# A decoder trunk on one core: two rows of a head's values moved behind the scores, and another order of the short and the long product in every wide block

## The chip, the cores and the metric

The kernel runs on one core of a Trainium2 chip. The metric is the device time of one execution in microseconds (us), as the median of several runs. Lower is better. The engines are named as the profile names them: PE is TensorE (its matmuls), PEld its weight loads, DVE is VectorE, ACT is ScalarE, POOL is GpSimd, SP is the engine whose queue issues most of the transfers.

## What is computed

A trunk of two layers over 256 tokens of width 1024, all in float32. Layer 0 mixes the tokens with a gated short convolution, layer 1 with dilated window attention (three groups of eight heads of 128, with partial rotary embedding). Each layer then has a squared-ReLU MLP (1024 to 4096 and back) and a gated per-layer input. Cut to what matters:

```python
for i in range(DEPTH):                                   # DEPTH = 2
    hn = rmsnorm(h, norm_mix[i])
    mixed = short_conv_mixer(...) if i == 0 else dilated_attention_mixer(hn, positions, w_qkv, w_o)
    h = h + mixed
    h = h + squared_relu_mlp(rmsnorm(h, norm_mlp[i]), mlp_w_up[i], mlp_w_down[i])
    h = h + sigmoid(rmsnorm(h, norm_ple[i]) @ ple_w_gate[i]) * (p[i] @ ple_w_proj[i])
return rmsnorm(h, norm_final)

def dilated_attention_mixer(h, positions, w_qkv, w_o):   # 3 groups g, 8 heads, 128 wide
    q, k, v = split(h @ w_qkv); q, k = partial_rotary(q), partial_rotary(k)
    for g: scores over a dilated window, softmax, times v, log of the sum
    return (softmax over the groups of those logs, times the outputs, summed) @ w_o
```

## The kernel before

Every float32 operand is split into a high and a low part of type fp32r, and a product of two such operands is made of three products: low weight by high activation, high weight by high activation, high weight by low activation. The weights stream from HBM in slabs (`raw`), ACT rounds a slab to its high part (`whi`, L368), DVE subtracts that to get the low part (`wlo`, L307), several slabs ahead of their use.

The work stands in a plan, a list that `make_plan` writes out by hand. An entry is a block of products of one 128x128 weight tile (or one slice of a row of them) or a step ("do") such as the rotary embedding or the softmax. `block` issues the matmuls of one entry (L404). There are three kinds:

- `"w"`, a *wide* block, is two matmuls. The weights are stationary. One streams the 256 columns of the activation's high part against `wlo` (below: the *short product*, S, a row with 128x256). The other streams 512 columns, high part and low part side by side, against `whi` (the *long product*, L, 128x512). The two halves of the bank are added up later by `add_up`, with one ACT and one DVE instruction for each half of a pair.
- `"n"` is three short products, all of 256 columns, for the few places that add up nothing later.
- `"t"` has the activations stationary and streams weight columns, 384 of them for a head's values (`acc_v`, a row with 128x384), 512 in the last stage.

Wide blocks come in twos, `half` 0 and 1 (the two column tiles of a pair of 128). Before the change the order of the two products follows `half`: S L for 0, L S for 1, so a stretch of wide blocks reads S L L S S L L S. Only the first group's queries and keys (g = 0) of heads 1 to 7 have S L in both halves:

```python
products = products[::-1] if half and (key != "qkv" or col[1] or not col[2]) else products
```

Head h of the attention is, in the plan: queries and keys of group 0 (`acc_qk`, 16 wide blocks); `scores` of head h-1, with the products of head h-2's values (`sc`, `o`, `tp` are the tiles of scores, of probabilities times values, and of the transposed probabilities); groups 1 and 2 of the queries and keys; `turn`, which transposes the probabilities of head h-1; eight rows of products for the values of head h (`v(h, ks)`, k from 0 to 7, six products of 384 columns each), with `qk_out` of group 2 and `qk_split` between them; `v_out`, which empties the two banks of the values. Head 1 differs: its `scores` come at group 2 and its `turn` behind the values ("late"). Head 7's scores come between blocks of the output projection (`w_o`).

PSUM has eight banks in one pool; a wide block's pair takes two, a head's values two, the scores two. Instructions run on each engine in the order that a scheduler gives them, which follows the plan, with a priority for some steps.

Of the kernel before, what the change touches and what calls it, by code (L numbers as in the profile page):

```python
# [18 lines left out]
NK = D // P  # L19
NP = NK // 2  # L20
FF = 4 * D
# [120 lines left out]
def make_plan():  # L142
    plan = [("do", "begin")]
    plan += proj_plan()

    def conv_in(what, c, ks):
        s = "BCX".index(what)
        return [
            ("w" if c and (what, c) != ("B", 3) or what == "X" else "n", "sc_in", k, s * NK + 2 * c + i, (what, c), i, "x0")
            for k in ks for i in (0, 1)  # L150
        ]


    for kp in range(NP):
        for what in "CBX":
            plan += conv_in(what, 0, (2 * kp, 2 * kp + 1))
            if what == "C" and kp + 1 < NP:
                plan.append(("do", "x_in", kp + 1))
            if what == "B":
                plan.append(("do", "squares", 0, kp))  # L160
    plan.append(("do", "add_up", ("X", 0)))
    for c in range(1, NP):
        plan += conv_in("C", c, range(2))
        plan += [("do", "stat", 0)] if c == 1 else []
        plan += conv_in("C", c, range(2, NK)) + ([("do", "add_up", ("C", c))]) + conv_in("X", c, range(3))
        plan += [("do", "spread", 0), ("do", "conv", 0)] if c == 1 else []
        plan += conv_in("X", c, range(3, NK)) + [("do", "add_up", ("X", c))] + conv_in("B", c, range(NK))
        plan.append(("do", "conv", c))

    def mix(key, j, ks):  # L170
        return [("w", key, k, 2 * j + i, ("o", j), i, "y") for k in ks for i in (0, 1)]

    for k in range(6):
        plan += mix("sc_out", 0, (k,)) + mix("sc_out", 1, (k,))

    plan += mix("sc_out", 2, range(3))
    for j in range(NP):
        plan += mix("sc_out", j, range((6, 6, 3, 0)[j], NK)) + [("do", "mix_out", 0, j)]
    plan += mlp_plan(0) + gate_plan()

    plan.append(("do", "masks"))

    def qk(h, g, ks):
        return [
            ("w", "qkv", k, (i, g, h), ("qk", h, g), i, "x3") for k in ks for i in (0, 1)
        ]

    def v(h, ks):
        return [("t", "v", k, h, ("v", b, h), b, "x3") for k in ks for b in (0, 1)]

    for kp in range(NP):
        for g in range(GROUPS):
            for k in (2 * kp, 2 * kp + 1):
                plan += qk(0, g, (k,))
                if (k, g) == (NK - 2, 0):
                    plan.append(("do", "stat", 3))
    plan += [("do", "add_up", ("qk", 0, g)) for g in (2, 0, 1)]
    plan += v(0, (0, 1)) + [("do", "spread", 3)]
    plan += [("do", "qk_out", 0, g) for g in (2, 0, 1)] + v(0, range(2, NK)) + [("do", "v_out", 0)]

    for h in range(1, HEADS):

        late, scores, turn = h == 1, [("do", "scores", h - 1)], [("do", "turn", h - 1)]
        for g in range(GROUPS):
            plan += qk(h, g, range(3)) + ([("do", "qk_out", h, g - 1)] if g else []) + qk(h, g, range(3, NK))
            if g == 0:
                plan += [("do", "qk_split", 0)] if late else scores
            elif g == 2:
                plan += scores if late else turn
            plan += [("do", "add_up", ("qk", h, g))]  # L210
        plan += v(h, range(2)) + [("do", "qk_out", h, 2)] + v(h, range(2, 4)) + [("do", "qk_split", h)]
        plan += v(h, range(4, NK)) + (turn if late else []) + [("do", "v_out", h)]

    last = HEADS - 1

    def w_o(kj):

        return [
            ("w" if j < 3 else "n", "w_o", k, 2 * j + i, ("o", j), i, "y") for k, j in kj for i in (0, 1)
        ]  # L220


    plan += w_o((k, j) for k in range(5) for j in (0, 1)) + [("do", "scores", last)]
    plan += w_o([(5, 0), (5, 1)] + [(k, 2) for k in range(6)] + [(0, 3), (1, 3)]) + [("do", "turn", last)]
    plan += w_o((k, 3) for k in range(2, 6)) + [("do", "last_values")]
    for j in range(NP):
        plan += w_o([(6, j), (7, j)]) + [("do", "mix_out", 1, j)]
    plan += mlp_plan(1) + [("do", "last_load")] + last_plan()
    return plan
# [36 lines left out]
def tile_trunk(ctx: ExitStack, tc: tile.TileContext, plan, slabs, ap, out):  # L266
# [51 lines left out]
    h = [held("h", f"h{j}", NP + 1) for j in range(NP)]  # L318
    state = {k: {} for k in ("u", "y", "p0", "p1", "qk", "pT", *(f"x{n}" for n in range(6)))}
    acc, left, opened = {}, {}, set()  # L320
    for op in plan:
        if op[0] != "do":
            key = ((*op[4], op[5]), 0) if op[0] == "w" else (op[4], op[5] if op[0] == "n" else 0)
            left[key] = left.get(key, 0) + 1
    rstd, rows, cur, mask, by_token = {}, {}, {}, {}, {}

    def gain(n, k):
        return gains[:, n * NK + k : n * NK + k + 1]
# [2 lines left out]
    offsets, n = [], 0  # L331
# [47 lines left out]
    def block(kind, key, k, col, name, half, operand, m=0, cuts=1):  # L379
        name = (*name, half) if kind == "w" else name  # L380
        if name not in opened:
            acc[name] = bank("acc_" + "_".join(map(str, name)))
        left[name, half if kind == "n" else 0] -= 1
        whi, wlo = weights((key, k, col))
        x = state[operand][k // 2]
        if kind == "n":
            dst = acc[name][:, half, :]
            products = ((dst, wlo, x[0][:, k % 2, :]), (dst, whi, x[1][:, k % 2, :]), (dst, whi, x[0][:, k % 2, :]))

            products = (products[2], products[0], products[1]) if key == "proj0" else products  # L390
        elif kind == "w":

            dst = acc[name]
            products = ((dst[:, 0, :], wlo, x[0][:, k % 2, :]), (flat(dst), whi, flat(x[2][:, k % 2, :, :])))

            products = products[::-1] if half and (key != "qkv" or col[1] or not col[2]) else products
        else:
            n = width(key) * P // cuts
            whi, wlo = (t[:, m * n : (m + 1) * n] for t in (whi, wlo))
            dst = flat(acc[name])[:, :n]  # L400
            xhi, xlo = (t[:, k % 2, half * P : (half + 1) * P] for t in x[:2])
            products = ((dst, xhi, whi), (dst, xhi, wlo), (dst, xlo, whi))
        for n, (to, a, b) in enumerate(products):
            nc.tensor.matmul(  # L404
                to,
                a,
                b,
                start=n == 0 and name not in opened,
                stop=n == len(products) - 1 and left[name, half if kind == "n" else 0] == 0,
                skip_group_check=True,  # L410
            )
            opened.add(name)
# [269 lines left out]

    def scores(head):

        weights = cur["pr", head] = pair(f"sm{head}", dtype=F32)[2]
        ps = [psum.tile([P, 512], F32, tag="ps", name=f"sc{head}_{b}") for b in (0, 1)]
        rest = values(head - 1) if head else None
# [265 lines left out]
```

## Time and profile before

| | |
|---|---|
| median of 3 runs | 771.32 us (771.22 to 771.48) |
| the profiled execution | 771.19 us |
| its span in the trace | 769.4 us |
| PE busy | 761.2 us (99%), 4716 matmuls |
| DVE busy | 598.6 us (78%) |
| ACT busy | 488.7 us (64%) |
| POOL busy | 8.9 us (1%) |
| moved from HBM | 138.97 MB read |

A matmul's row in the timeline has its start, its duration and its tiles. Matmuls are pipelined, so durations overlap: an S lasts 0.28 us and an L 0.40 us in the rows, but the next one starts earlier. What counts for the time is the distance from one start to the next start, called the *pitch* below. It is read from two rows of the timeline and the count of matmuls between them.

### The profile page before, as it was taken

To read this page: it belongs to the slowest core of one execution; us is meant where nothing else is said; L and a number is where in the kernel's file an instruction comes from. 1 tells how busy PE (TensorE), PEld (TensorE's weight loads), DVE (VectorE), ACT (ScalarE), POOL (GpSimd) and SP (SyncE) were. 2 spreads that over 40 slices of the span, in tenths; PEclk is the share of its full clock that TensorE was granted. 3 is DMA by queue.
4 is the path that set the end of the run, shared out by engine and by line. 5 is a ranking of instruction groups with operands and counts; after the bars stand their busy time and mean duration, and the time that the engine had idled before them with its cause. 6 is when DMAs were issued, how large, how long until landed. Compare 5 with 4: busy or idle time off the path is not lost.

```text
span 769.4 us, 12415 instructions
## 1 busy us (share of the span) xinstructions
PE 761.2 (99%) x4716; PEld 680.2 (88%) x4716; DVE 598.6 (78%) x967; ACT 488.7 (64%) x796; POOL 8.9 (1%) x22
## 2 busy tenths in 40 slices
PE   9999999999999999999999999999999999999996
PEld 9988888888888899989989989989988888888885
DVE  6898789898566668898988978977899887655564
ACT  7765566666444446688887778777666555444453
POOL 0000000000000000000000000000000000000002
PEclk9999999999999999999999999999999999999999
DMA  8855555556555554554555456456465555555521
GB/s 311 312 190 192 195 191 169 190 190 197 188 190 191 192 191 139 191 187 152 169 171 197 152 162 200 147 160 219 138 192 188 193 191 191 187 188 189 184 90 56
DMA packets 42539, 140.83 MB, mean 183 GB/s; under 512 B 4848, under 2 KB 6384, under 8 KB 42480
## 3 DMA queue, kind: packets, MB, share of 16 engines
q1 hardware_dynamic: 41904, 139.39, 54.3%
q8 instruction: 37, 0.61, 0.3%
q10 hardware_dynamic: 576, 0.66, 0.3%
q14 instruction: 22, 0.18, 0.1%
HBM read 138.97 MB, written 1.05 MB: 182 GB/s over the span
## 4 chain that ended last, share of the span: by engine, by line
PE 97%; issue 1%; DMA 1%; DVE 0%; POOL 0%; SPq 0%; POOLq 0%; ACT 0%; DVEq 0%
PE acc_u L404 23%; PE acc_d L404 23%; PE acc_qk L404 18%; PE acc_v L404 9%; PE acc_o L404 6%; PE acc_g L404 5%; PE acc_B L404 3%; PE acc_C L404 3%; PE acc_X L404 3%; PE acc_p L404 1%; PE o L736 1%; PE sc L692 1%; PE o L746 1%; DMA raw<-in_w 1%; PE sc L700 1%
## 5 line engine op out<-in xcount | busy, mean ns | idle before, releaser
L307 DVE TENSOR_TENSOR wlo<-raw,whi 128x1024 fp32r<-128x1024 f32 (+2 forms) x277 | 319.2, 1155 | 126.4 <-ACT whi L368 123.9
L368 ACT ACTIVATE whi<-raw 128x1024 fp32r<-128x1024 f32 (+2 forms) x277 | 277.9, 1007 | 166.2 <-PE acc_d L404 77.1
L404 PE MATMUL acc_u<-x,whi 128*128 128x512 f32 x512 | 160.8, 396 | 0.0
L404 PE MATMUL acc_d<-u,whi 128*128 128x512 f32 x512 | 160.8, 395 | 0.0
L404 PE MATMUL acc_qk<-x,whi 128*128 128x512 f32 x384 | 124.6, 395 | 0.0
L404 PEld LDWEIGHTS acc_d<-u,wlo 128*128 128x128 f32 x512 | 96.2, 188 | 22.7
L404 PEld LDWEIGHTS acc_u<-x,wlo 128*128 128x128 f32 x512 | 96.0, 188 | 22.5
L404 PE MATMUL acc_u<-x,wlo 128*128 128x256 f32 x512 | 101.3, 278 | 0.0
L404 PE MATMUL acc_d<-u,wlo 128*128 128x256 f32 x512 | 100.9, 278 | 0.0
L404 PE MATMUL acc_qk<-x,wlo 128*128 128x256 f32 x384 | 86.9, 280 | 0.0
L404 PEld LDWEIGHTS acc_qk<-x,wlo 128*128 128x128 f32 x384 | 72.1, 188 | 12.1
L404 PEld LDWEIGHTS acc_u<-x,whi 128*128 128x128 f32 x512 | 78.0, 189 | 0.2
L404 PEld LDWEIGHTS acc_d<-u,whi 128*128 128x128 f32 x512 | 77.9, 189 | 0.0
L404 PE MATMUL acc_v<-whi,x 128*128 128x384 f32 x256 | 67.2, 337 | 0.0
L404 PEld LDWEIGHTS acc_qk<-x,whi 128*128 128x128 f32 x384 | 62.5, 188 | 4.6
L404 PEld LDWEIGHTS acc_v<-whi,x 128*128 128x128 f32 x256 | 46.5, 188 | 0.1
L404 PE MATMUL acc_v<-wlo,x 128*128 128x384 f32 x128 | 42.9, 335 | 0.0
L423 ACT ACTIVATE r<-acc_u 128x256 f32<-128x256 f32 x64 | 24.1, 378 | 27.8 <-PE acc_u L404 27.5
L404 PE MATMUL acc_o<-y,whi 128*128 128x512 f32 (+1 forms) x144 | 41.0, 370 | 0.0
L655 ACT ACTIVATE rot<-qk 16x512 f32<-16x512 f32 x48 | 30.3, 632 | 9.9 <-DVE qk L424 9.2
L424 DVE TENSOR_TENSOR r<-acc_u,r 128x256 f32<-128x256 f32 x64 | 26.5, 419 | 3.5 <-ACT r L423 3.0
L404 PEld LDWEIGHTS acc_o<-y,wlo 128*128 128x128 f32 x128 | 24.0, 188 | 5.0
(175 smaller groups left out, 976.4 us busy)
## 6 DMA issues: line engine op xcount, KB each, us to landing
raw<-in_w SPq DMA_DIRECT2D x230, 512.0 KB, 3.6
raw<-in_w SPq DMA_DIRECT2D x32, 384.0 KB, 3.4
raw<-in_w SPq DMA_DIRECT2D x10, 256.0 KB, 4.9
h<-in_xT SPq DMA_DIRECT2D x4, 256.0 KB, 5.0
gain<-in_gain SPq DMA_DIRECT2D x2, 256.0 KB, 4.6
out<-htg SPq DMA_DIRECT2D x2, 256.0 KB, 2.1
mask<-in_mask SPq DMA_DIRECT2D x2, 192.0 KB, 3.4
raw<-in_w ACTq DMA_DIRECT2D x2, 128.0 KB, 3.7
```

Of the source, the lines that this page charges most:

```text
L307: nc.vector.tensor_tensor(out, a, f32(b), ALU.subtract)
L368: nc.scalar.activation(hi[:, :width], t[:, :width], AF.Copy)
L404: nc.tensor.matmul(to, a, b, start=n == 0 and name not in opened, stop=n == len(products) - 1 and left[name, half if kind == "n" else 0] == 0,
L423: nc.scalar.activation(t[:, i, :], p[:, 1, :], AF.Copy)
L424: nc.vector.tensor_tensor(t[:, i, :], p[:, 0, :], t[:, i, :], ALU.add)
L655: nc.scalar.activation(r[dst : dst + 16], p[src : src + 16], AF.Copy)
L692: nc.tensor.matmul(ps[b][:, :S], q[:, 0, own], k[:, 1, :], start=n == 0, stop=n == 2)
L700: nc.tensor.matmul(ps[b][r * 64 : (r + 1) * 64, at : at + 64], t[:, 0, of], t[:, 1, of], start=True, stop=True)
L736: nc.tensor.matmul(ps[:, 0, :], a, b[:, kb, :], start=kb == 0 and n == 0, stop=False, skip_group_check=True)
L746: nc.tensor.matmul(ps[to, 0, q], v12[:, b, r * P + m * 64 : r * P + (m + 1) * 64], t[:, b, r * 64 : (r + 1) * 64], start=False, stop=n == ...
```

## The change

It does four things.

1. `block` keeps a counter `wide_run`. A wide block with counter 0 issues S L; every later one issues L S. A block of kind `"n"` and the step `scores` set the counter to 0, a block of kind `"t"` sets it to a large number. So behind short products a stretch reads S L, L S, L S, L S: one pair of neighbours in opposite orders, and then alternation. Behind a head's values it reads L S, L S from the start.
2. From head 2 on, the rows k = 0 and 1 of a head's values move from behind group 2 to directly behind `scores`, ahead of group 1. Head 1 keeps them where they were.
3. `qk_out` of group 2 now stands behind row 2 and `qk_split` behind row 4 of the values (before: behind rows 1 and 3).
4. `add_up` of a group of queries and keys is asked for ahead of `scores` or `turn`, not behind.

```diff
         for g in range(GROUPS):
             plan += qk(h, g, range(3)) + ([("do", "qk_out", h, g - 1)] if g else []) + qk(h, g, range(3, NK))
+            plan += [("do", "add_up", ("qk", h, g))]
             if g == 0:
-                plan += [("do", "qk_split", 0)] if late else scores
+
+                plan += [("do", "qk_split", 0)] if late else scores + v(h, range(2))
             elif g == 2:
                 plan += scores if late else turn
-            plan += [("do", "add_up", ("qk", h, g))]
-        plan += v(h, range(2)) + [("do", "qk_out", h, 2)] + v(h, range(2, 4)) + [("do", "qk_split", h)]
-        plan += v(h, range(4, NK)) + (turn if late else []) + [("do", "v_out", h)]
+        plan += (v(h, range(2)) if late else []) + v(h, (2,)) + [("do", "qk_out", h, 2)] + v(h, (3, 4)) + [("do", "qk_split", h)]
+        plan += v(h, range(5, NK)) + (turn if late else []) + [("do", "v_out", h)]
...
         x = state[operand][k // 2]
+        if kind != "w":
+
+            wide_run["n"] = 0 if kind == "n" else NK * FF
...
-            products = products[::-1] if half and (key != "qkv" or col[1] or not col[2]) else products
+
+            done = wide_run.get("n", 0)
+            wide_run["n"] = done + 1
+            products = products[::-1] if done % 2 or done > 1 else products
...
     def scores(head):
 
+        wide_run["n"] = 0
```

How it moves the rows of PE, at three places. First, inside the down projection of the MLP (`acc_d_1_0` and `acc_d_1_1` are the banks of the two halves, `u5` the activations, `whi85` and `wlo85` a slab's parts). Before:

```order
L404 MATMUL acc_d_1_0_2374<-u5_1592,wlo85_2295 128x256
L404 MATMUL acc_d_1_0_2374<-u5_1592,whi85_2294 128x512
L404 MATMUL acc_d_1_1_2383<-u5_1592,whi85_2294 128x512
L404 MATMUL acc_d_1_1_2383<-u5_1592,wlo85_2295 128x256
L404 MATMUL acc_d_1_0_2374<-u5_1592,wlo85_2295 128x256
L404 MATMUL acc_d_1_0_2374<-u5_1592,whi85_2294 128x512
L404 MATMUL acc_d_1_1_2383<-u5_1592,whi85_2294 128x512
L404 MATMUL acc_d_1_1_2383<-u5_1592,wlo85_2295 128x256
```

The same eight places after:

```order
L411 MATMUL acc_d_1_0_2374<-u5_1592,whi85_2294 128x512
L411 MATMUL acc_d_1_0_2374<-u5_1592,wlo85_2295 128x256
L411 MATMUL acc_d_1_1_2383<-u5_1592,whi85_2294 128x512
L411 MATMUL acc_d_1_1_2383<-u5_1592,wlo85_2295 128x256
L411 MATMUL acc_d_1_0_2374<-u5_1592,whi85_2294 128x512
L411 MATMUL acc_d_1_0_2374<-u5_1592,wlo85_2295 128x256
L411 MATMUL acc_d_1_1_2383<-u5_1592,whi85_2294 128x512
L411 MATMUL acc_d_1_1_2383<-u5_1592,wlo85_2295 128x256
```

No matmul is added or removed; two long products never stand next to each other now, nor two short ones. Second, PE where the convolution's output projection (`acc_o`) begins behind three-product blocks (`acc_B_3`), after the change:

```order
L411 MATMUL acc_B_3_945<-x0_3_376,whi34_846 128x256 x2
L411 MATMUL acc_o_0_0_1024<-y0_571,wlo35_870 128x256
L411 MATMUL acc_o_0_0_1024<-y0_571,whi35_869 128x512
L411 MATMUL acc_o_0_1_1033<-y0_571,whi35_869 128x512
L411 MATMUL acc_o_0_1_1033<-y0_571,wlo35_870 128x256
L411 MATMUL acc_o_1_0_1036<-y0_571,whi35_869 128x512
L411 MATMUL acc_o_1_0_1036<-y0_571,wlo35_870 128x256
L411 MATMUL acc_o_1_1_1039<-y0_571,whi35_869 128x512
L411 MATMUL acc_o_1_1_1039<-y0_571,wlo35_870 128x256
```

The first two blocks stand as before the change (S L L S), and from the third on every block reads L S. Third, PE behind the scores of head 2 (`sc2`), where head 3 goes on. Before:

```order
L700 MATMUL sc2_1_4247<-qk_2_2_4098 64x64 x2
L404 MATMUL acc_qk_3_1_0_4296<-x3_0_3093,wlo147_4131 128x256
L404 MATMUL acc_qk_3_1_0_4296<-x3_0_3093,whi147_4130 128x512
L404 MATMUL acc_qk_3_1_1_4305<-x3_0_3093,whi147_4130 128x512
L404 MATMUL acc_qk_3_1_1_4305<-x3_0_3093,wlo147_4131 128x256
```

After:

```order
L708 MATMUL sc2_1_4252<-qk_2_2_4100 64x64 x2
L411 MATMUL acc_v_0_3_4296<-whi147_4125,x3_0_3093 128x384
L411 MATMUL acc_v_0_3_4296<-wlo147_4126,x3_0_3093 128x384
...
L411 MATMUL acc_v_1_3_4306<-wlo147_4126,x3_0_3093 128x384
L411 MATMUL acc_v_1_3_4306<-whi147_4125,x3_0_3093 128x384
L411 MATMUL acc_qk_3_1_0_4316<-x3_0_3093,whi148_4148 128x512
L411 MATMUL acc_qk_3_1_0_4316<-x3_0_3093,wlo148_4149 128x256
```

Twelve products of the values (two rows) now stand between the 64-column matmuls of the scores and group 1, which begins with a long product.

More of the change, by code (lines that the diff above doesn't have):

```diff
@@ L324, in tile_trunk @@
             left[key] = left.get(key, 0) + 1
-    rstd, rows, cur, mask, by_token = {}, {}, {}, {}, {}
+    rstd, rows, cur, mask, by_token, wide_run = {}, {}, {}, {}, {}, {}
     def gain(n, k):
```

## The prediction

> **What bounds the kernel now.** I read the page first, for the engine that bounds, then the waits, then the timeline of PE for pitches. Lines of the page (busy time, granted clock, the chain that ended last):
>
> ```profile
> span 769.4 us, 12415 instructions
> PE 761.2 (99%) x4716; PEld 680.2 (88%) x4716; DVE 598.6 (78%) x967; ACT 488.7 (64%) x796; POOL 8.9 (1%) x22
> PEclk9999999999999999999999999999999999999999
> PE 97%; issue 1%; DMA 1%; DVE 0%; POOL 0%; SPq 0%; POOLq 0%; ACT 0%; DVEq 0%
> ```
>
> PE is the path from end to end, at full clock. Next, the waits: of PE alone (the first line is the whole answer), and two lines of the list for all engines (us in total, times, longest):
>
> ```profile
> PE warm L531 <- DVE power L527: 1.0, 1, 1.0
> ...
> DVE wlo L307 <- ACT whi L368: 123.9, 122, 2.7
> ACT whi L368 <- PE acc_d L404: 77.1, 46, 2.0
> ```
>
> PE waited visibly for another engine only before its first matmul. The weight splitters wait the other way round: DVE for ACT (123.9 us), ACT for PE to free a slab (77.1 us). So the time is the number of matmuls times their pitch, and a change of order is worth what it does to the pitch. How many blocks there are, from the groups by shape (count behind the x, then busy us and mean ns):
>
> ```profile
> L404 PE MATMUL acc_u<-x,whi 128*128 128x512 f32 x512 | 160.8, 396 | 0.0
> L404 PE MATMUL acc_d<-u,whi 128*128 128x512 f32 x512 | 160.8, 395 | 0.0
> L404 PE MATMUL acc_qk<-x,whi 128*128 128x512 f32 x384 | 124.6, 395 | 0.0
> ...
> L404 PE MATMUL acc_o<-y,whi 128*128 128x512 f32 x112 | 35.1, 395 | 0.0
> ...
> L404 PE MATMUL acc_X<-x,whi 128*128 128x512 f32 x64 | 20.1, 395 | 0.0
> ...
> L404 PE MATMUL acc_C<-x,whi 128*128 128x512 f32 x48 | 15.1, 395 | 0.0
> ...
> L404 PE MATMUL acc_B<-x,whi 128*128 128x512 f32 x32 | 10.1, 395 | 0.0
> ```
>
> Each wide block has one long product: 512 + 512 + 384 + 112 + 64 + 48 + 32 = 1664 blocks. Group 0 of heads 1 to 7 (7 x 16 = 112) alternates already; 1552 blocks get a new order.
>
> Now the pitches. The timeline's rows begin with start and duration in us. First the down projection of layer 0 (first row of it, first row behind it), then group 0 of heads 3 and 4, likewise, which are the stretches that alternate before the change:
>
> ```profile
> 191.34 0.28 PE L404 MATMUL acc_d<-u,wlo 128*128 128x256 f32 x1
> ...
> 280.51 0.28 PE L404 MATMUL acc_g<-x,wlo 128*128 128x256 f32 x1
> ...
> 385.47 0.33 PE L404 MATMUL acc_v<-whi,x 128*128 128x384 f32 x1
> 385.65 0.28 PE L404 MATMUL acc_qk<-x,wlo 128*128 128x256 f32 x1
> 385.76 0.40 PE L404 MATMUL acc_qk<-x,whi 128*128 128x512 f32 x1
> ...
> 391.20 0.51 PE L736 MATMUL o<-pT,v 128*128 128x256 f32 x3
> ...
> 413.84 0.28 PE L404 MATMUL acc_qk<-x,wlo 128*128 128x256 f32 x1
> ...
> 419.39 0.63 PE L736 MATMUL o<-pT,v 128*128 128x256 f32 x4
> ```
>
> S L L S: 256 blocks in 280.51 - 191.34 = 89.17 us, 348.3 ns a block. Alternation: 16 blocks in 5.55 us, both times, 346.9 ns a block (the rows' last digit leaves +-0.6). To sharpen that, the pitches of unmixed streams: short products alone (the gate of layer 0, 102 of them up to `acc_qk`) and long ones alone (45 in the last stage):
>
> ```profile
> 292.19 0.28 PE L404 MATMUL acc_g<-x,wlo 128*128 128x256 f32 x1
> ...
> 304.43 0.28 PE L404 MATMUL acc_qk<-x,wlo 128*128 128x256 f32 x1
> 304.55 0.63 PE L404 MATMUL acc_qk<-x,whi 128*128 128x512 f32 x2
> 305.02 0.39 PE L404 MATMUL acc_qk<-x,wlo 128*128 128x256 f32 x2
> ...
> 750.50 0.39 PE L404 MATMUL acc_p<-whi,p 128*128 128x512 f32 x1
> ...
> 760.70 0.28 PE L404 MATMUL acc_p<-whi,p 128*128 128x256 f32 x1
> ```
>
> S alone: 12.24 us / 102 = 120.0 ns. L alone: 10.20 us / 45 = 226.7 ns. Their sum is 346.7 ns, just what alternation shows: alternating costs nothing over the two streams by themselves, and S L L S costs 1.6 ns more, some bubble at its doubled neighbours.
>
> **The change, part by part.**
>
> *The order.* 1552 blocks x (348.3 - 346.7) = 2.5 us gained. By 346.9 it is 2.2 us, which is the low end of a full gain; I take 346.7, since the sum of two long stretches is measured more finely than 16 blocks. The counter starts again at nine places (four times in the first convolution blocks, at the convolution's output projection, the first queries, twice in the attention's output projection, at the MLP of layer 1), and each keeps one doubled pair, half of what a period S L L S has: 9 x 1.6 ns = 0.01 us.
>
> Here a page speaks against the change. The Trainium skill, "TensorE: Matmul & The Clock Gate", section "Back-to-back issue gap", gives the isolated gap of a warm matmul as N/2.4 + 2.5 ns, a function of the columns alone. By it an S and an L take 109 and 216 ns (an estimate from that page) in any order, the order is free, and this term would be 0 in place of -2.5 us. The rows disagree in size (120.0 and 226.7) and show two prices for two orders.
>
> *New borders in the heads.* From head 2 on (six heads) the 64-column matmuls of the scores are followed by a value product and not by an S. Both borders stand in the trace, the first in head 1, the second in head 3:
>
> ```profile
> 348.54 0.45 PE L404 MATMUL acc_v<-whi,x 128*128 128x384 f32 x1
> 348.82 0.34 PE L404 MATMUL acc_v<-wlo,x 128*128 128x384 f32 x1
> ...
> 393.79 0.39 PE L404 MATMUL acc_qk<-x,wlo 128*128 128x256 f32 x1
> 394.01 0.63 PE L404 MATMUL acc_qk<-x,whi 128*128 128x512 f32 x2
> ```
>
> The first value product takes 0.28 us to the next start, 0.10 over the 0.18 of 385.47 to 385.65; the first S takes 0.22, 0.10 over its 0.12. So the exchange costs 0, with 0.02 for the rounding. The border from values to a *long* product is new: 13 times (group 1 of heads 2 to 7, group 0 of heads 1 and 3 to 7, the output projection behind head 7). No row shows it. Above, it is bounded by the 0.10 us of the border from 64 columns (1.3 us in all); below by the border from values to S, which costs 0 (385.47, 385.65, 385.76: pitches 0.18 and 0.11). It is nearest to the latter, as the products ahead are the same: I take 0.01 each, 0.13 us.
>
> *Less time for the chains on DVE and ACT.* Only two rows less of values (12 x 0.175 = 2.1 us) stand between `turn` and the use of the transposed probabilities; between `qk_split` and the scores it is one row (1.05 us). How much room there is, from the list by tile (duration min/median/max, first and last start; head 3's stretch):
>
> ```profile
> L736 PE MATMUL o<-pT,v x6: 274/281/282, 419.4 to 420.0; 128*128 128x256 f32 x6
> ...
> L307 DVE TENSOR_TENSOR pT<-tp,pT x1: 684/684/684, 407.4 to 407.4; 128x512 fp32r<-128x512 f32 x1
> ...
> L307 DVE TENSOR_TENSOR qk<-qk,qk x1: 684/684/684, 408.7 to 408.7; 128x512 fp32r<-128x512 f32 x1
> ```
>
> The probabilities are ready at 408.1 and used at 419.4: 11.3 us, of which 9.2 stay. The split queries and keys are ready at 409.4 for scores near 420: 10.6, of which 9.5 stay. The softmax gets 2.1 us more before `turn`. Cost 0. The two banks of the values are held over groups 1 and 2 too: a head then opens 12 banks of 8 as before, in another order. `add_up` earlier in DVE's and ACT's order frees its banks earlier; behind it stand the softmax and the copy of the output, which have those 9 us and more. The slab with value rows 0 and 1 is loaded and split four slabs earlier and queries' slabs one later: same count, same bytes, the SP queue in the new order of use. Cost 0; if the cover of 9 us were gone, the scores' consumers on PE would wait.
>
> *One place where PE does wait.* At the MLP of layer 1, the pair of long products behind 553.94 takes 0.57 us to the next start, against 0.47 at 304.55:
>
> ```profile
> 553.78 0.28 PE L404 MATMUL acc_u<-x,wlo 128*128 128x256 f32 x1
> 553.94 0.73 PE L404 MATMUL acc_u<-x,whi 128*128 128x512 f32 x2
> 554.51 0.40 PE L404 MATMUL acc_u<-x,wlo 128*128 128x256 f32 x2
> ```
>
> It waits for the activations, which DVE makes from the last output projection. What PE gains between the two is waited for again: at most some 32 blocks (8 of `acc_o`, 24 of `acc_u`) x 1.6 ns = 0.05 us.
>
> **Sum.** -2.5 + 0.01 + 0.12 (six exchanges at 0.02) + 0.13 + 0.05 = -2.2 us. The profiled execution took 771.19 us (span 769.4 and 1.8 around it): 769.0. The median of the runs is 0.13 higher; I say 769.1.
>
> **The rivals.**
>
> 1. *The order is free, or the bubble comes back with the other order.* An S and an L have their pitch, the 1.6 ns belong to the stage and not to the order, and the alternating stretches are cheap because values stand ahead of them. Against it: in the same heads, groups 1 and 2 are S L L S, on the same operands. Result 0 plus borders: 771.3 to 771.6. Chance 0.07. (This is what the rule of the Trainium skill's TensorE page, above, would make of the change.)
> 2. *Only a part settles.* The statistics' matmuls inside the MLPs (two short ones between `acc_u` blocks) are followed by alternation without a doubled pair; if the stream stays disturbed there, the second half of the up projections and all of the down projections (768 blocks) gain nothing. 768 x 1.6 ns = 1.2 us are missing then: 770.3. Head 2's group 0 speaks against it, which alternates behind four transposes. Chance 0.07.
> 3. *Slower: alternation locks in behind short products.* Behind S alone (304.43 to 305.02) the S takes 120 ns and each L 235: 355 a block. In S L L S this is made good, since the second S of a pair is cheaper. If S 120 with L 235 repeats without end, 1328 blocks (all but groups 1 and 2 of heads 1 to 7, which follow values) cost 6.7 ns more: 8.9 us, less 0.4 for the others, 0.3 for the borders: 780.1. It turns into a loss at a mean block above 348.3 ns. For it: alternation is seen only behind values and transposes, never behind S. Against it: the one doubled pair comes first, and both entries that are seen fall to 346.9 within a head. Chance 0.06.
> 4. *A wait in the heads.* The 9 us of room would have to go, in six heads; it begins to cost when DVE falls that far behind. Each us over is 6 us in all. Chance 0.02, price 772 to 776.
>
> **How the numbers follow.** The forecast has 0.78. Its own range: from -2.5 with free borders (768.8) to -2.2 by the 16-block reading, with all borders at their upper bound (0.05 + 0.12 + 1.3: 770.6, which I think unlikely). With 0.3 for the runs' own spread, the range that is to hold 8 in 10 takes in rival 2 and the borders' bound, 768.4 to 770.9; rivals 1, 3 and 4 (0.15) stay out. A difference under 0.2% (1.5 us) can't be told from none: faster means below 769.8. Faster 0.76 (the forecast, less 0.02 for its upper end), same 0.16 (rivals 1 and 2 and those 0.02), slower 0.08 (rivals 3 and 4).
>
> **What the profile after would show.** The down projection's 256 blocks in 88.75 us (346.7 each) and not 89.17, in both layers: this decides between forecast and rivals 1 to 3, and 90.9 would be rival 3. The up projection's halves before and behind the statistics' matmuls apart: rival 2. From values to a long product: a pitch of the last value product near 0.17 and of the first L near 0.23, with 0.33 for the upper bound. PE still with one wait, before its first matmul; any other is rival 4. I am wrong if the state of the stream behind short products outlives one pair, or if the bubble belongs to something other than doubled neighbours.

## The result

The changed kernel took 777.19 us (median; 774.99 to 777.42) against 771.40 us for the kernel before on the same chip: 1.0070 times as long, 95% interval 1.0056 to 1.0084. Slower by 0.7%, where 769.1 us and a gain of 0.3% were forecast. Three of the four executions took 777.2 to 777.4 us and one 774.99. The profiled one, on which all stage times below rest, took 777.18 us.

From the page of the changed kernel, span, busy time, granted clock and the chain's shares:

```profile
span 775.4 us, 12420 instructions
PE 766.5 (99%) x4716; PEld 682.9 (88%) x4716; DVE 598.8 (77%) x967; ACT 484.0 (62%) x796; POOL 8.9 (1%) x22
PEclk9999999999999999999999999999999999999999
PE 93%; DVE 3%; issue 2%; ACT 1%; DMA 1%; POOL 0%; SPq 0%; POOLq 0%; DVEq 0%; ACTq 0%
```

PE has the same 4716 matmuls at the same clock, is as busy as before (99%), and the span is 6.0 us longer: mostly, the pitch grew. The down projections, first row of each and first row behind it, in layer 0 and in layer 1:

```profile
192.64 0.40 PE L411 MATMUL acc_d<-u,whi 128*128 128x512 f32 x1
...
283.09 0.28 PE L411 MATMUL acc_g<-x,wlo 128*128 128x256 f32 x1
...
648.09 0.40 PE L411 MATMUL acc_d<-u,whi 128*128 128x512 f32 x1
...
738.54 0.40 PE L411 MATMUL acc_g<-whi,x 128*128 128x512 f32 x1
```

256 blocks in 90.45 us, twice: 353.3 ns a block, where S L L S had 348.3 and the forecast had 346.7. Inside one of them, and then in group 1 of head 3, which follows values:

```profile
193.34 0.40 PE L411 MATMUL acc_d<-u,whi 128*128 128x512 f32 x1
193.58 0.28 PE L411 MATMUL acc_d<-u,wlo 128*128 128x256 f32 x1
193.70 0.40 PE L411 MATMUL acc_d<-u,whi 128*128 128x512 f32 x1
193.94 0.28 PE L411 MATMUL acc_d<-u,wlo 128*128 128x256 f32 x1
194.05 0.40 PE L411 MATMUL acc_d<-u,whi 128*128 128x512 f32 x1
194.28 0.28 PE L411 MATMUL acc_d<-u,wlo 128*128 128x256 f32 x1
194.40 0.40 PE L411 MATMUL acc_d<-u,whi 128*128 128x512 f32 x1
...
398.54 0.33 PE L411 MATMUL acc_v<-whi,x 128*128 128x384 f32 x1
398.71 0.39 PE L411 MATMUL acc_qk<-x,whi 128*128 128x512 f32 x1
398.94 0.28 PE L411 MATMUL acc_qk<-x,wlo 128*128 128x256 f32 x1
399.06 0.39 PE L411 MATMUL acc_qk<-x,whi 128*128 128x512 f32 x1
```

In the down projection the L takes 0.24, 0.24, 0.23 us and the S 0.12, 0.11, 0.12, and this cycle of three blocks (1.06 us) repeats to the end. Behind values an L takes 0.23 and an S 0.12 at once, and stays there: 31 blocks at 346.7 ns. So alternation has two cycles, a *fast* one (346.7) and a *slow* one (353.3), and a stretch keeps the one it falls into until something interrupts it. S L L S lies between them, at 348.3. The kind of products ahead doesn't settle which: the 106 blocks of the first convolution behind `spread` (36.77 us) are fast too, and group 0 of head 2, behind four transposes, was fast before the change (346.7 ns from its third block) and is slow after it. In the changed kernel's trace the long stretches in the slow cycle hold 1153 blocks (17 of the first convolution columns, 190 from the convolution's output projection to the MLP's statistics, 384 from there to the end of the down projection, 36 of the first queries, 15 in head 2, 126 and 385 in layer 1). 1153 x 5.0 ns (353.3 - 348.3) = 5.8 us. By the stages below, those that are slow throughout lost 5.7 us together and the attention's output projection 1.0, while the heads gained 0.4 and what stands ahead of the convolution's output projection 0.3; this makes the 6.0.

By stage, worked out from the starts of matmuls (us from a stage's first matmul to the next stage's; profiled executions; s and f are the cycle, - is S L L S):

| stage | before | after |
|---|---|---|
| convolution's output projection | 22.29 - | 22.60 s |
| up projection 0, ahead of / behind the statistics | 44.59 - / 44.83 - | 45.23 s / 45.46 s |
| down projection 0 | 89.17 - | 90.45 s |
| first queries and keys | 17.19 - | 17.39 s |
| heads 1 to 7 | 196.19 | 195.75 f (group 0 of head 2: s) |
| attention's output projection | 27.17 | 28.17 |
| up projection 1, ahead / behind | 44.76 - / 44.83 - | 45.52 s / 45.46 s |
| down projection 1 | 89.17 - | 90.45 s |

The attention's output projection is a second loss, 1.0 us. The list of PE's waits has a new line there, for half of it:

```profile
PE o L744 <- DVE pT L308: 0.5, 1, 0.5
```

### The profile page after: what moved, and what is told of

It reads as the page before. It is cut to its first block, busy times and chain, and to the rows that moved or that the text cites. A ratio compares the mean times of both kernels' runs of the same rounds, so it can differ in the third digit from the quotient of the medians.

```text
span 775.4 us, 12420 instructions
## 1 busy us (share of the span) xinstructions
PE 766.5 (99%) x4716; PEld 682.9 (88%) x4716; DVE 598.8 (77%) x967; ACT 484.0 (62%) x796; POOL 8.9 (1%) x22
## 4 chain that ended last, share of the span: by engine, by line
PE 93%; DVE 3%; issue 2%; ACT 1%; DMA 1%; POOL 0%; SPq 0%; POOLq 0%; DVEq 0%; ACTq 0%
PE acc_u L411 23%; PE acc_d L411 23%; PE acc_qk L411 17%; PE acc_v L411 8%; PE acc_g L411 5%; PE acc_o L411 4%; PE acc_B L411 3%; PE acc_C L411 3%; PE acc_X L411 3%; DVE wlo L308 1%; PE acc_p L411 1%; PE o L744 1%; PE sc L700 1%; PE o L754 1%; DMA raw<-in_w 1%
## 5 line engine op out<-in xcount | busy, mean ns | idle before, releaser
L411 PE MATMUL acc_u<-x,whi 128*128 128x512 f32 x512 | 181.1, 399 | 0.0
L411 PE MATMUL acc_d<-u,whi 128*128 128x512 f32 x512 | 181.0, 399 | 0.0
L411 PE MATMUL acc_u<-x,wlo 128*128 128x256 f32 x512 | 143.8, 281 | 0.0
L411 PE MATMUL acc_d<-u,wlo 128*128 128x256 f32 x512 | 143.8, 281 | 0.0
L411 PE MATMUL acc_qk<-x,whi 128*128 128x512 f32 x384 | 134.2, 393 | 0.0
L411 PEld LDWEIGHTS acc_d<-u,whi 128*128 128x128 f32 x512 | 96.2, 188 | 24.0
L411 PEld LDWEIGHTS acc_u<-x,whi 128*128 128x128 f32 x512 | 96.1, 188 | 24.1 <-DVE x L455 0.2
L411 PE MATMUL acc_qk<-x,wlo 128*128 128x256 f32 x384 | 107.6, 280 | 0.0
L411 PE MATMUL acc_o<-y,wlo 128*128 128x256 f32 x128 | 35.7, 283 | 0.0
L683 ACT ACTIVATE v<-acc_v,n 64x128 f32<-64x128 f32 x64 | 23.2, 362 | 12.4 <-DVE v L679 11.7
```

The lines of the kernel that those rows point to most:

```text
L411: nc.tensor.matmul(to, a, b, start=n == 0 and name not in opened, stop=n == len(products) - 1 and left[name, half if kind == "n" else 0] == 0,
L683: nc.scalar.activation(v12[to, b, r * P : (r + 1) * P], p[own, g * P : (g + 1) * P], AF.Copy, scale=scale[own])
```

## The experiments

All ratios are to the kernel before on the same chip, with 95% intervals. The theories are first those that the result suggested, then the one that remained. In the expectations o0 and o1 are the output projections of the convolution and of the attention, and pT7 is the tile of head 7's transposed probabilities.

**The moved rows without the order.** After's plan, before's rule of order:

```diff
-            products = products[::-1] if done % 2 or done > 1 else products
+            products = products[::-1] if half and (key != "qkv" or col[1] or not col[2]) else products
```

> The change of the plan alone (value rows behind the scores, add_up and qk_split moved), with the order of products of before: S L L S everywhere, S L in group 0. Theory A (alternation of short and long products has two states, 346.7 and 353.3 ns a block; the changed kernel is in the slow one in the output projections, the MLPs and the first queries; the move costs nothing): 771.0 to 771.7 us, ratio 0.999 to 1.001, down projections at 89.17 us. Theory B (the moved rows or the waits behind them make the loss): 774 us or more.

Measured: 771.29 us, 1.0001 (0.9992 to 1.0010); behind the first matmuls of the convolution no stage of its trace differs from before by more than 0.02 us. The move alone costs nothing, in the heads and in the output projection.

**The doubled pair.** Three rules in place of after's: S L everywhere but behind values (no pair), L S everywhere, and two pairs ahead of the alternation.

```diff
-            products = products[::-1] if done % 2 or done > 1 else products
+            products = products[::-1] if done >= NK * FF else products      # e2
+            products = products[::-1] if True else products                 # e3
+            products = products[::-1] if done % 2 or done > 3 else products # e4
```

> As the changed kernel, but behind short products (and behind head 7's scores) every block is S L from the first on: no doubled pair. Theory A with the state set by the stream of short products ahead, whatever follows: 353.3 ns a block again, 90.45 us a down projection, 776.5 to 777.5 us. Theory A with the state set by the doubled pair L L: 346.7 ns, 88.75 us a down projection, 768.5 to 770 us. Rival (S L and L S differ as such, whatever stands ahead): the fast state wherever S L stands, the slow one nowhere, 768.5 to 770 us, and group 0 behind values no different from before.

> As the changed kernel, but every wide block is L S, with no doubled pair behind short products. Theory A, state set by the short products ahead: 353.3 ns a block, 776.5 to 777.5 us. Theory A, state set by the doubled pair: 346.7 ns, 768.5 to 770 us. Either way the heads behind values stay at 346.7.

> As the changed kernel, but with two doubled pairs (S L L S S L L S) behind short products before L S goes on. If the number of matmuls between the last short product and the alternation decides the state (a phase that each doubled pair shifts): the fast state, 346.7 ns, 88.75 us a down projection, 768.5 to 770 us. If the doubled pair has no part in it: 353.3 ns, 776.5 to 777.5 us as the changed kernel.

Measured: 774.16 us, 1.0050 (1.0031 to 1.0068); 777.25, 1.0074 (1.0059 to 1.0089); 775.33, 1.0055 (1.0040 to 1.0070). The whole MLP of layer 0 is in the slow cycle in all three: no pair, one or two at its start, S or L first, makes no difference there. But layer 1 differs, so that the totals of e2 and e4 lie in neither of the ranges expected. Its down projection is fast in e2 and e4, slow in e3. The two down projections of e2:

```profile
192.98 0.28 PE L411 MATMUL acc_d<-u,wlo 128*128 128x256 f32 x1
...
283.43 0.28 PE L411 MATMUL acc_g<-x,wlo 128*128 128x256 f32 x1
...
646.75 0.28 PE L411 MATMUL acc_d<-u,wlo 128*128 128x256 f32 x1
...
735.49 0.40 PE L411 MATMUL acc_g<-whi,x 128*128 128x512 f32 x1
```

The same instructions on the same shapes, 90.45 us and 88.74 us. So the cycle isn't fixed by the order, the shapes or the kind of stream ahead alone. In layer 1 the up projection can begin behind a wait of PE for the activations (0.2 us in e3); no trace has such a wait in layer 0. The executions of one kernel differ as well: 774.02 to 777.62 us in e2, 775.53 to 777.75 in e3, 774.99 to 777.42 after the change, where those of the kernel before lie within 1.1 us in each comparison. From the statistics of layer 1 to the end of its down projection the slow cycle costs 2.5 us over the fast one (45.46 + 90.45 against 44.61 + 88.75, in e3 and e2), so layer 1 falling now into one, now into the other would fit; each kernel has one profile, so this is not shown. What remained was a theory: the cycle depends on *when*, within the cycle, a stretch is entered, and an interruption can shift it.

**Added products of other widths.** `kick` issues a few matmuls whose output is not used; the stretch behind it begins with L.

```diff
+    def kick():
+        wide_run["n"] = NK * FF
+        ps = flat(bank("kick"))
+        for _ in range(N):
+            nc.tensor.matmul(ps[:, :W], ones_r, cur["slab"][:, :W], start=True, stop=True)
```

It stands ahead of the convolution's output projection, behind `spread` of that mixer (e5 to e8), ahead of the first queries (e9 to e12), behind the statistics of both MLPs, and ahead of the MLP of layer 1. Each run has its kick at all of its five places.

> The changed kernel with one extra product of 384 columns (its result is not used) at five places: ahead of the convolution's output projection, behind the spread of the first statistics, behind the statistics inside each MLP, ahead of layer 1's MLP; L S from there. Theory A1 (the state is set by the kind of stream ahead, and a product longer than its weight load puts it in the fast state): up projections behind the statistics 44.6 us and down projections 88.75 us in both layers, -7.2 us and +0.9 for the extra products, 770.5 to 771.5 us. Theory A2 (the state hangs on the exact distance in time, whatever the kind): some stretches fast, some slow, 771 to 777 us.

> As the kernel with one extra product of 384 columns, but three in a row at each of the five places (+2.6 us). A1: all five stretches fast, 772 to 773 us, the down projections 88.75 us. A2: mixed again, and not the same stretches as with one.

> Three extra products of 512 columns at each of the five places (+3.4 us). A1: all fast as behind 384 columns, 773 to 774 us. If the head's values do it by 384 columns alone and not by length: slow or mixed, 775 to 780.5 us.

> Three extra short products (256 columns) at each of the five places (+1.8 us), the control. A1: slow, as behind other short products: the down projections 90.45 us, 778 to 779.5 us. A2 or any disturbance will do: some or all fast, 771.5 to 777 us.

> The changed kernel with one extra product of 128 columns (result not used) at five places: ahead of the convolution's output projection, of the first queries, of layer 1's MLP, and behind the statistics inside each MLP; L S from there. So far every stretch that follows a long stream of short products at 120 ns was slow, also with one or three products of 384 or 512 columns between; those all have pitches that are whole multiples of 13.33 ns (120, 173.3, 226.7). Theory A3 (what counts is a phase in time that such products leave as it is, and that a product bound by its weight load, some 110 ns, shifts): fast in the convolution's output projection (22.3 us or less from there to the first up projection) and in most other stretches, 769 to 772 us. Theory A1 (kind of stream ahead): slow, 777 to 778 us.

> The same with 64 columns: by A3 another shift than with 128, so fast or slow stretch by stretch, 769 to 776 us; a stretch that starts behind the steady 120 ns stream has the same state in both layers' like places. By A1: slow, 777 to 778 us.

> Two products of 128 columns at each place: by A3 twice the shift; if one made a stretch fast by half a period of 13.33 ns, two bring it back to slow in the convolution's output projection; 769 to 777 us. By A1: slow, 777 to 778 us.

> One product of 320 columns at each place, longer than its weight load; its pitch should be 146.7 ns (halfway between 120.0 and 173.3), again a whole multiple of 13.33 ns. By A3: no shift, the convolution's output projection and the first queries slow as behind 384 columns (22.6 us, 17.4 us), 772 to 775 us. If any product that is not of 256, 384 or 512 columns frees the stream: fast.

Measured, with the cycle in each stretch of the profiled execution (the down projection always keeps that of the up projection's second half; "mixed" is explained below):

| kick | us | ratio | conv. output, up 0 | behind statistics 0 | first queries | up 1 | behind statistics 1 |
|---|---|---|---|---|---|---|---|
| none (after) | 777.19 | 1.0070 (1.0056 to 1.0084) | s | s | s | s | s |
| 1 x 64 | 772.33 | 1.0013 (1.0003 to 1.0022) | s | f | s | mixed | f |
| 1 x 128 | 777.46 | 1.0079 (1.0061 to 1.0097) | s | s | s | mixed | s |
| 2 x 128 | 776.77 | 1.0059 (1.0038 to 1.0080) | f | s | f | s | s |
| 1 x 320 | 772.47 | 1.0015 (1.0006 to 1.0025) | s | f | s | mixed | f |
| 1 x 384 | 772.55 | 1.0016 (1.0007 to 1.0026) | s | f | no kick, s | mixed | f |
| 3 x 384 | 774.58 | 1.0042 (1.0027 to 1.0057) | s | f | no kick, s | mixed | f |
| 3 x 256 | 773.52 | 1.0030 (1.0019 to 1.0041) | s | f | no kick, s | s | f |
| 3 x 512 | 777.03 | 1.0075 (1.0058 to 1.0091) | s | f | no kick, s | mixed | s |

The down projection of layer 0 with one product of 384 columns behind the statistics:

```profile
192.63 0.39 PE L414 MATMUL acc_d<-u,whi 128*128 128x512 f32 x1
...
281.37 0.28 PE L414 MATMUL acc_g<-x,wlo 128*128 128x256 f32 x1
```

88.74 us: a single product 45 us ahead settles 384 blocks. But neither width nor number decides by itself. One 384 does it behind the statistics and not ahead of the convolution's output projection, so "values reset the stream" falls as a rule. Three short products (256) do it behind the statistics, so the kind of product ahead (A1) falls too. Two of 128 do it in the two places where nothing else did, and fail behind the statistics, where one of 64 does it; three of 512 do it there in layer 0 and not in layer 1. No size is right everywhere: this is how a phase would behave. But A3, which said which sizes shift it, missed: by it one of 128 should have freed the convolution's output projection, and two should have left it slow. It was the other way round. The up projection of layer 0 up to the statistics, after the change and with two of 128 ahead of the projection before it:

```profile
101.95 0.40 PE L411 MATMUL acc_u<-x,whi 128*128 128x512 f32 x1
...
147.18 0.39 PE L510 MATMUL ssq<-sums,ones_r 128*128 128x256 f32 x2
```

```profile
102.21 0.39 PE L415 MATMUL acc_u<-x,whi 128*128 128x512 f32 x1
...
146.58 0.40 PE L514 MATMUL ssq<-sums,ones_r 128*128 128x256 f32 x2
```

45.23 and 44.37 us.

The column of layer 1's first stretch (up 1) needs care. Where it says mixed, the kick did not settle the stretch: in PE's order one short product stands 24 blocks later than its partner, so that two long ones meet early in the stretch and two short ones later. The cycle changes at such places and only there. With one product of 64 columns:

```profile
558.81 0.62 PE L415 MATMUL acc_u<-x,whi 128*128 128x512 f32 x2
559.27 0.28 PE L415 MATMUL acc_u<-x,wlo 128*128 128x256 f32 x1
...
567.40 0.40 PE L415 MATMUL acc_u<-x,wlo 128*128 128x256 f32 x2
567.64 0.40 PE L415 MATMUL acc_u<-x,whi 128*128 128x512 f32 x1
...
600.23 0.40 PE L514 MATMUL ssq<-sums,ones_r 128*128 128x256 f32 x2
```

From 559.27 to 567.40 there are 23 blocks at 353.3 ns, and from 567.64 to the statistics 94 at 346.7: the stretch was slow behind its kick, and the two short products side by side moved it. e13, e17, e18 and e3, which has no kick, have the same displaced product, and e2 turns fast behind three short ones in a row (563.23); the kernel after, e4, e14 and e15 do not, and are slow up to the statistics. So a doubled pair inside a stretch can change its cycle.

**All places at once.** If the cycle is a matter of each entry, the kicks that worked must add up: two of 128 ahead of the convolution's output projection and the first queries, one of 64 behind the statistics (and ahead of the MLP of layer 1, where the trace above gives it no part). e13 has them in after's kernel, e17 on before's plan (no rows moved). In both the attention's output projection keeps before's order.

```diff
+    plan += [("do", "kick", 2, 128)]   # ahead of the two projections
+            plan.append(("do", "kick"))   # 1 x 64, behind stat_rows of the MLPs
+    plan += [("do", "kick")] + mlp_plan(1) + ...
-            products = products[::-1] if done % 2 or done > 1 else products
+            products = products[::-1] if (half if key == "w_o" else done % 2 or done > 1) else products
```

> After's kernel with added matmuls in the places and sizes that moved a stretch into the fast state one at a time before: two of 128 columns ahead of the convolution's output projection and ahead of the first queries, one of 64 behind the statistics of both MLPs and ahead of the MLP of layer 1; the attention's output projection keeps before's order. Theory (the state is set by the phase at which a stretch is entered, place by place, so that the places add up): o0 22.24 us, up projection 44.4 and 44.7, down 88.75, first queries 17.15, heads 195.75, so 1.7 us less than before from these, and o1 between 27.2 and 28.1: 769.6 to 770.6 us. Rival (the states depend on more than the entry, so that one kick moves what follows another): at least one of the down projections or up projections of layer 0 is slow again, 771.5 or more.

> As e13_both_kicks, but on before's plan. Theory (phase per place, and the wait for pT7 comes from the moved rows with the new DVE order): all stretches fast, o1 27.2 to 27.4: 769.5 to 769.9, faster than before by about 0.2%. Rival (states not additive): 771.5 or more. If o1 is 28 here too, the moved rows have nothing to do with the wait: 770.5.

Measured: e13 770.84 us, 0.9995 (0.9986 to 1.0003); e17 770.86, 0.9995 (0.9986 to 1.0004). In both, these stages took to 0.01 us what they had taken in the run with that kick (e11 or e10): convolution's output projection 22.24, up projection 0 44.38 and 44.72, down projection 0 88.75, first queries 17.15, and in layer 1 from the statistics on 44.72 and 88.75. The down projections of e13:

```profile
190.88 0.39 PE L415 MATMUL acc_d<-u,whi 128*128 128x512 f32 x1
...
279.62 0.28 PE L415 MATMUL acc_g<-x,wlo 128*128 128x256 f32 x1
...
643.16 0.39 PE L415 MATMUL acc_d<-u,whi 128*128 128x512 f32 x1
...
731.90 0.39 PE L415 MATMUL acc_g<-whi,x 128*128 128x512 f32 x1
```

So the cycle of each stretch can be set at its own entry, whatever was set elsewhere. This also shows that the loss was the slow cycle: with seven matmuls added e13 takes 6.3 us less than the changed kernel, in the same order but for the entries and the attention's output projection; e3, without a doubled pair at the entries, and e14 below, with that projection's order, gain nothing by these alone (777.25 and 777.05 us). The theory of the entry stands; that it is a phase which counts there is inferred. The totals were 0.2 us (e13) and 1.0 us (e17) above the expected ranges, for two reasons: in e13 the output projection kept its wait (28.44 us), and in e17 heads 1 to 7 took 196.89 us, for which the next run has the cause.

**The order without the moved rows**, and after's kernel with before's order in the output projection alone:

```diff
-                plan += [("do", "qk_split", 0)] if late else scores + v(h, range(2))   # e15: before's plan
+                plan += [("do", "qk_split", 0)] if late else scores
...
-            products = products[::-1] if done % 2 or done > 1 else products              # e14
+            products = products[::-1] if (half if key == "w_o" else done % 2 or done > 1) else products
```

> Before's plan (no rows of values moved) with after's rule of order: the order alone. Theory (the whole loss is the order; the move only takes room from the chain on DVE): slow behind short products as in after, heads 195.7 us, o1 without the wait for pT7 at 27.2 or so: 775.9 to 776.5, or up to 2.7 less if layer 1 enters fast. Rival (the moved rows cost by themselves in the new order): 774.5 or less with layer 1 still slow.

> After's kernel, but the wide blocks of the attention's output projection in before's order. It asks where the 0.48 us wait for pT7 in that projection comes from. Theory A (DVE is later in all heads from 2 on, since a weight split now stands ahead of the softmax, and this shows behind head 7): the wait stays, o1 at 27.9 to 28.3 us, in all 776.9 to 777.4. Theory B (the order inside the output projection makes the wait): o1 back at 27.2, in all about 776.2. If the MLP of layer 1 happens to enter fast, 1 to 2.7 us less in both.

Measured: e15 774.84 us, 1.0052 (1.0037 to 1.0068), with single executions from 774.00 to 777.58; e14 777.05, 1.0075 (1.0059 to 1.0090). In e15 the heads took 196.89 us, 0.70 more than before. Its group 1 of head 3, which now follows the 64-column matmuls of the scores:

```profile
397.35 0.40 PE L410 MATMUL acc_qk<-x,whi 128*128 128x512 f32 x1
397.58 0.28 PE L410 MATMUL acc_qk<-x,wlo 128*128 128x256 f32 x1
397.70 0.40 PE L410 MATMUL acc_qk<-x,whi 128*128 128x512 f32 x1
397.94 0.28 PE L410 MATMUL acc_qk<-x,wlo 128*128 128x256 f32 x1
398.06 0.40 PE L410 MATMUL acc_qk<-x,whi 128*128 128x512 f32 x1
398.30 0.28 PE L410 MATMUL acc_qk<-x,wlo 128*128 128x256 f32 x1
398.41 0.40 PE L410 MATMUL acc_qk<-x,whi 128*128 128x512 f32 x1
```

The slow cycle again, in groups 1 and 2 of heads 3 to 7 (those of head 2 fell into the fast one). So the moved rows do something, but only with the new order: they set the fast cycle in the heads, worth 196.89 - 195.75 = 1.14 us. My expectation of 195.7 for e15 was a miss. Layer 1 of e15 is slow up to its statistics and fast behind them, with no kick at all, where after stays slow: the same order of matmuls, another outcome.

The wait for `pT` is unchanged in e14 (28.17 us), so it doesn't come from the order inside the output projection. It is absent in e15 (27.23) and in e1 (27.17). It takes the moved rows and the new order together. What is late is DVE. The last matmuls of head 7's scores and the first step of its softmax, after the change and in e1:

```profile
537.91 0.64 PE L708 MATMUL sc<-qk 128*64 128x64 f32 x16
539.95 0.55 DVE L715 CUSTOM_DVE_ANT_0 sm<-sc,mask 128x384 f32<-128x384 f32 x1
```

```profile
535.97 0.64 PE L708 MATMUL sc<-qk 128*64 128x64 f32 x16
536.42 0.56 DVE L715 CUSTOM_DVE_ANT_0 sm<-sc,mask 128x384 f32<-128x384 f32 x1
```

2.04 against 0.45 us. DVE's and ACT's instructions around there stand in the same order in both; for heads 2 to 6 the new order of the matmuls led the scheduler to put a weight split ahead of a head's rotation and softmax. How much of the delay comes from that wasn't separated.

**The last head.** As e13, but head 7 keeps its rows of values where before has them:

```diff
-        late, scores, turn = h == 1, ...
+        late, stay, scores, turn = h == 1, h in (1, HEADS - 1), ...
-                plan += ... else scores + v(h, range(2))
+                plan += ... else scores + ([] if stay else v(h, range(2)))
-        plan += (v(h, range(2)) if late else []) + ...
+        plan += (v(h, range(2)) if stay else []) + ...
```

> As e13_both_kicks, but head 7 keeps its rows of values where before has them; heads 2 to 6 have them behind the scores. Theory (the wait for pT7 comes from moved rows together with the new order in the last head alone; and moved rows are worth 1.14 / 6 = 0.19 us a head in the new order): heads 195.94 us, o1 27.4 without a wait on PE, all else as in e13: 770.84 + 0.19 - 1.02 = 770.0 us. Rival (DVE is late from all the heads before): the wait stays in o1, 771.0 us.

Measured: 770.25 us, 0.9989 (0.9980 to 0.9998), the fastest of all; its interval just leaves out 1. A gain of 0.1% in one comparison, the best of many, is weak evidence. PE's waits are one line again:

```profile
PE warm L542 <- DVE power L538: 1.0, 1, 1.0
```

Heads 195.97 us (expected 195.94), output projection 27.73 (expected 27.4). So most of the wait belongs to the last head's moved rows. A rest is left: the list for `pT` still has the weight load of `o` behind it, 0.3 us (0.7 in e13, none in e17, whose output projection takes 27.42).

## Why the prediction was wrong

- *What bounds the kernel* was right: PE's pitch, at full clock, and a change of order is worth what it does to the pitch.
- *The order, -2.5 us*: this step failed. It gave 346.7 ns to all 1552 blocks, from stretches that follow values or transposes. In 1138 of them, most behind short products, and in 15 of head 2's group 0, the same alternation took 353.3: 1153 x 5.0 ns = +5.8 us. Even the sharper figure, the sum of S alone and L alone, misled: it gave the fast cycle exactly, and said nothing on whether a stretch enters it.
- *Rival 3* was the mechanism: alternation locks in behind short products. Its place was right, and its price nearly: I took S 120 and L 235 (355 ns) from one pair of blocks, and the cycle is three blocks of 1060 ns together (353.3). At that price and 1153 blocks in place of 1328 it would have given 777; that this meets the measured time is partly luck, since it has no term for the 1.0 us of the output projection. "Behind short products" isn't the rule, though: some stretches behind other products are slow, and some behind short ones fast. What I set against it, that the doubled pair comes first, was an argument without a row; in e2 to e4 a pair at the entry makes no difference in layer 0. That both entries seen had fallen to 346.9 was evidence from other entries, and one of the two, head 2's group 0, is slow after the change, behind the same transposes. A chance of 0.06 was too low for a case that the trace could neither show nor exclude.
- *Rival 2* had its place right: the statistics are an entry of their own, and what is entered there lasts to the end of the down projection; but it is the slow cycle, not the price of S L L S. Head 2's group 0, which I set against it, was no witness, as said.
- *Rival 1* falls: the order is not free. The Trainium skill, "TensorE: Matmul & The Clock Gate", section "Back-to-back issue gap", gives the isolated gap of a warm matmul as a function of its columns. In the streams here the same columns have three prices, 346.7, 348.3 and 353.3 ns a block.
- *Borders in the heads*: held. From values to L the pitch is 0.17 us (398.54 to 398.71) and the first L takes 0.23, the low end that I took; the heads gained 0.44 us.
- *Less time for the chains on DVE and ACT, 0*: wrong by 0.5 (the wait listed) to 1.0 us (the stage), behind head 7 alone. *Rival 4* looked for such a wait in six heads and so at another place and price. I took the room of a middle head (11.3 us) for all. Behind head 7 there is less to hide behind, and DVE's own order changed, which I had not taken from the changed kernel's lists.
- *Moved rows*: I gave them no effect of their own on the pitch. They were worth 1.14 us in the new order.

## What to carry to other kernels

When PE runs back to back, the price of an order of long and short matmuls is not a number but depends on how the stretch is entered, and it lasts: read it from a stretch with the same entry, or measure that entry, before multiplying by a thousand blocks. An order that holds an irregularity in each period (S L L S here) had one price, 348.3 ns, in both MLPs, 0.5% above the best and 1.4% below the worst; it is a sound choice where the entries can't be controlled. And a change of order on one engine can make the scheduler reorder the others: look at their chains at the last repetition, where the cover ends.

## What the runs showed of the hardware

The alternation of 512 and 256 columns has two self-sustaining cycles, 346.7 and 353.3 ns a block, and keeps one over 384 blocks (136 us) and across the border from the up to the down projection. One product of 64 columns behind the statistics can move it from the one to the other (e10), and so can two short products side by side inside the stretch (e10, layer 1). Unmixed streams take 120.0 ns (256 columns) and 226.7 ns (512), which are 9 and 17 times 13.33 ns, and the slow cycle's excess over three blocks, 1060 - 1040 = 20 ns, is one and a half of that; this is arithmetic, and no run shows a clock of that length. What in the engine holds the cycle is open, and that it is a phase is inferred from how kicks move it. Why two products of 128 columns work behind short products, and one of 64, 320 or 384 (but not of 128) behind the statistics, is not explained either; but the same kicks gave the same cycles at these places in e13, e17 and e18.
